# Strassen's seven products in the input projection of a hybrid decoder layer

## The chip, the cores and the metric

The kernel runs on one core of a Trainium2 chip. The metric is the device time of one execution in microseconds. Engines are named as in the profile: PE is TensorE, DVE is VectorE, ACT is ScalarE, POOL is GpSimd, SP is SyncE, whose queue issues the DMA transfers.

## The reference

One layer: a root-mean-square norm of x (1024 tokens by 2048 channels), one combined input projection, three groups of attention heads that read it, a gate on each, an output projection, the residual and a last norm.

```python
h = rmsnorm(x, norm_g) @ w_in
(c_q, c_kv, k_rope, z_mla, q_nsa, k_c, v_c, k_s, v_s, k_w, v_w, g_nsa, z_nsa,
 q_mem, z_mem) = jnp.split(h, offsets, axis=-1)
o_mla = mla_mixer(c_q, c_kv, k_rope, ...) * jax.nn.silu(z_mla)
o_nsa = nsa_mixer(q_nsa, k_c, v_c, k_s, v_s, k_w, v_w, g_nsa, ...) * jax.nn.silu(z_nsa)
o_mem = memory_mixer(q_mem, mem, mem_norm_g, w_mem_kv) * jax.nn.silu(z_mem)
o = jnp.concatenate([o_mla, o_nsa, o_mem], axis=-1) @ w_out
return rmsnorm(x + o, final_norm_g)
```

The projection to 40 feature tiles of 128 columns is what changes. (Some 268 columns that are needed with tokens on the partitions, the "nat" products, are made apart.)

## The kernel before

Every float32 product is made of three: an operand is split into a rounded part `hi` (ACT copies it, L116 or L118) and the remainder `lo` (DVE subtracts, L110 or L112), and `mm3` (L121 to L124) adds hi·hi, hi·lo and lo·hi in PSUM.

**Startup.** For each of the 16 channel tiles of x, ACT and DVE split it into one `big` buffer (16 buffers of 128x2048, all of which then hold x), ACT squares it (L194), POOL adds the square into `acc` (L195), and PE makes the nat products of 128x268. Then come the keys and values of 256 memory tokens, whose squares POOL adds to `macc` (L269). From `acc`, `col_rsqrt` and `spread` make `R`, the inverse norm of every token on all partitions (L229 is its last step).

**Feature tiles.** A loop runs over the 40 feature tiles. A tile takes 16 channel tiles, two halves of 512 tokens and three products: 96 matmuls of 128x512 (L561, `proj_k`) into two of four `S` banks. `wtile` loads half of the tile's weights (512 KB) and splits it; `evac` multiplies each bank by `R` on the way to one of four `work` buffers of 128x1024 (L569 to L573); a SiLU (L575), a split (`keep_split`) or nothing follows, and the result is stored in DRAM. The dictionary `side` lays other work behind given tiles: the compression branch (`kc_...`, `vc_...`), the norms and the scaling of the latent tiles (`c_sum`, `c_norm`, `c_scale`, L467 to L472, which takes two `work` buffers each), the rotary key and memory attention (`mem_...`).

**Order.** Each engine runs its instructions in a fixed order, which a list scheduler makes out of the program's order, the dependencies and the free buffers; SP issues every DMA in one queue. Behind the projection come the loads of the sparse attention: `ks` tiles, `kc`, `qn`, `qrh`, `ali`.

Of the kernel before, what the change touches and what calls it, by code (L numbers as in the profile page):

```python
# [43 lines left out]
def chunks(w):  # L44
    """How w score columns are cut: (first column, columns used, columns computed)."""
    if w <= 512:
        return [(0, w, max(w, 256))]
    f = 384 if w == 640 else 512
    return [(0, f, f), (f, w - f, w - f)]
# [3 lines left out]
def hybrid_block_kernel(ctx: ExitStack, tc, a, out):  # L53
# [16 lines left out]

    def whl():
        return (sb.tile([P, KW], F32R, tag="wh", bufs=4, name=nm("wh"))[:, :1024],
                sb.tile([P, KW], F32R, tag="wl", bufs=4, name=nm("wl"))[:, :1024])
# [47 lines left out]
    def mm3(dst, sh, sl, mh, ml, start, stop):  # L121
        PE.matmul(dst, sh, mh, start=start, stop=False)  # L122
        PE.matmul(dst, sh, ml, start=False, stop=False)  # L123
        PE.matmul(dst, sl, mh, start=False, stop=stop)  # L124

    def rsqrt(dst, v, s, dim):
        """dst = 1 / sqrt(v / dim + EPS); v is overwritten, s is scratch."""
# [17 lines left out]

    cd = [dram(f"c{j}", [P, SEQ]) for j in range(8)]
# [23 lines left out]
    def keep_split(o, dst, n=1024):  # L170
        """Split o and keep both parts in DRAM: dst = (place of hi, place of lo)."""
        hi, lo = work(F32R), work(F32R)
        split(hi[:, :n], lo[:, :n], o)
        store(dst[0], f(hi[:, :n]))
        store(dst[1], f(lo[:, :n]))

    # ------------------------------------------------ input projection
    xt = []
    acc = rs(F32)
    nat = [t[:, :268] for t in (psS(), psS(), psS(), psS(), psT(), psT(), psO(), psJ())]  # L180
    for c in range(8):
# [4 lines left out]
        for k in (2 * c, 2 * c + 1):  # L186
            xr = work()
# [3 lines left out]
            if k == 0:  # L191
                S.activation(acc, xr, AF.Square)
            else:
                S.activation(xr, xr, AF.Square)  # L194
                G.tensor_tensor(acc, acc, xr, op=ALU.add)  # L195
            xt.append(t)
# [6 lines left out]
    vw = [work(), work(), work()]  # L203
    for i in range(NQ):
        d = vw[i // 3][:, (i % 3) * 268:(i % 3) * 268 + 268]
# [6 lines left out]
    def col_rsqrt(col, sq, n, dim):  # L212
        """col[:, i] = the inverse norm of token tile i; sq holds sums of squares along partitions."""
# [5 lines left out]
    def spread(dst, col, n):  # L219
        """dst[:, token] = col of the token, on every partition."""  # L220
# [11 lines left out]
    R = rs(F32)  # L232
# [3 lines left out]
    def nat_out(n):  # L236
        i0 = 3 * n
        m = min(3, NQ - i0)
        for i in range(i0, i0 + m):
            d = vw[n][:, (i - i0) * 268:(i - i0) * 268 + 268]  # L240
            V.tensor_scalar(d, d, rcol[:, i:i + 1], None, op0=ALU.mult)
        v3 = vw[n][:, :m * 268].rearrange("p (i c) -> p i c", c=268)
        S.activation(gates[:, i0:i0 + m, :], v3[:, :, 256:268], AF.Sigmoid)
        hi, lo = whl()
        hi, lo = [t[:, :m * 256].rearrange("p (i c) -> p i c", c=256) for t in (hi, lo)]
        split(hi, lo, v3[:, :, :256])
        for b, dst in enumerate((vsd, vwd)):
            for o, t in ((0, hi), (1024, lo)):
                store(dst[:, o + i0 * P:o + (i0 + m) * P].rearrange("p (i c) -> p i c", c=P), f(t[:, :, b * P:b * P + P]))

    # ------------------------------------------------ memory tokens: keys and values
    macc = sb.tile([P, 256], F32, tag="z", bufs=2, name="macc")
    kps, vps = [psS() for _ in range(4)], [psJ(), psO()]
    for c in range(4):
# [7 lines left out]
        for t in range(4):  # L262
# [7 lines left out]
        for t in range(4):  # L270
            k = 4 * c + t
            wr = wraw()
            load(wr, a["w_mem"][k])
            wh, wl = whl()
            split(wh, wl, wr)
            q = slice(t * 256, t * 256 + 256)
            for h in range(4):
                mm3(kps[h][:, :256], wh[:, h * P:h * P + P], wl[:, h * P:h * P + P],
                    mh[:, q], ml[:, q], k == 0, k == 15)
            for i in range(2):  # L280
                o = t * 256 + i * P
# [1024 lines left out]
```

## Time and profile before

| | us |
|---|---|
| runs | 1959.21, 1960.35, 1960.33 |
| median | 1960.33 |
| span of the profiled execution | 1959.9 |
| projection (first to last L561 matmul) | 125.7 to 1062.9 |

The profiled execution's span, from the first instruction to the last, is 0.4 us below the median of the runs, so spans and times can be compared directly. PE is busy for 98% of the span; DVE, ACT and POOL for 46%, 36% and 9%. The page gives busy time by engine, the costliest groups of instructions with what ended the idle time before them, and the transfers; the trace behind it gives each instruction.

### The profile page before, as it was taken

The page shows a single profiled execution, that of the slowest core. Times are in us where ns is not written, and L with a number is a line of the kernel's source. Part 1 is how long each engine was busy: PE and PEld are TensorE (multiplying, and loading weights), DVE is VectorE, ACT ScalarE, POOL GpSimd, SP SyncE. Part 2 cuts the span into 40 slices and gives each one's busy share as a digit, 9 for nine tenths or more (in the row PEclk, how much of TensorE's full clock was granted, in tenths as well). Part 3 has the DMA queues.
Part 4 walks back from the last instruction along what each step waited for, and adds up shares of the span by engine and source line. Part 5 has one row for each costly group of instructions (what it writes and reads, how often), then busy time and mean ns, then how long its engine had stood idle before and what let it go on. Part 6 is the DMA issues. An engine that isn't in the chain of part 4 may idle for free. (4 is left out here: it accounts for less than half of the span.)

```text
span 1959.9 us, 26350 instructions
## 1 busy us (share of the span) xinstructions
PE 1913.3 (98%) x10174; PEld 1646.6 (84%) x10174; DVE 903.8 (46%) x1908; ACT 705.5 (36%) x1389; POOL 176.9 (9%) x306
## 2 busy tenths in 40 slices
PE   7899999999999999999999999999999999999998
PEld 7788887888888888888887998888998988888888
DVE  8742232333323223222212887858778782244342
ACT  6542231212222112233312666535445462243231
POOL 6400000000100000000000221200000001110120
PEclk9999999999999999999999999999999999999999
DMA  6564443346545243323226234442122165357332
GB/s 211 164 187 128 132 164 116 120 153 224 179 155 189 97 129 97 119 83 108 81 95 183 67 89 137 149 136 63 46 74 63 54 208 173 97 176 275 97 108 87
DMA packets 94683, 255.43 MB, mean 130 GB/s; under 512 B 12059, under 2 KB 37469, under 8 KB 91357
## 3 DMA queue, kind: packets, MB, share of 16 engines
q1 hardware_dynamic: 94557, 253.74, 40.2%
q8 instruction: 80, 1.31, 0.3%
q14 instruction: 46, 0.38, 0.1%
HBM read 190.76 MB, written 62.93 MB: 129 GB/s over the span
## 5 line engine op out<-in xcount | busy, mean ns | idle before, releaser
L561 PE MATMUL S<-big,wh 128*128 128x512 f32 x2560 | 688.9, 391 | 0.0
L561 PEld LDWEIGHTS S<-big,wh 128*128 128x128 f32 x2560 | 477.8, 188 | 97.0
L116 ACT ACTIVATE wh<-wraw 128x1024 fp32r<-128x1024 f32 (+2 forms) x192 | 196.9, 1028 | 711.0 <-PE S L561 393.9
L110 DVE TENSOR_TENSOR wl<-wraw,wh 128x1024 fp32r<-128x1024 f32 (+2 forms) x192 | 246.8, 1289 | 409.5 <-ACT wh L116 407.8
L561 PE MATMUL S<-big,wl 128*128 128x512 f32 x1280 | 396.0, 390 | 0.0
L561 PEld LDWEIGHTS S<-big,wl 128*128 128x128 f32 x1280 | 239.9, 188 | 49.9 <-issue 0.2
L573 DVE TENSOR_TENSOR work<-S,rs 128x512 f32<-128x512 f32 x60 | 38.7, 686 | 295.8 <-PE S L561 295.8
L122 PE MATMUL S<-wh,big 128*128 128x512 f32 (+2 forms) x336 | 122.1, 363 | 7.2 <-ACT big L118 7.2
L124 PE MATMUL S<-wh,big 128*128 128x512 f32 (+2 forms) x336 | 122.5, 365 | 5.3 <-DVE big L112 5.3
L123 PE MATMUL S<-wl,big 128*128 128x512 f32 (+2 forms) x336 | 122.0, 363 | 0.0
L497 ACT ACTIVATE work<-S,st 128x512 f32<-128x512 f32 (+3 forms) x148 | 84.5, 572 | 87.1 <-DVE st L704 33.0
L122 PEld LDWEIGHTS S<-wh,big 128*128 128x128 f32 x336 | 64.4, 192 | 16.6 <-ACT big L118 7.2
L124 PEld LDWEIGHTS S<-wh,big 128*128 128x128 f32 x336 | 64.5, 192 | 15.3 <-DVE big L112 5.8
L122 PE MATMUL O<-wh,big 128*128 128x256 f32 (+2 forms) x232 | 71.3, 307 | 1.2 <-ACT wh L116 1.2
L123 PEld LDWEIGHTS S<-wl,big 128*128 128x128 f32 x336 | 64.4, 192 | 9.3
L123 PE MATMUL O<-wl,big 128*128 128x256 f32 (+2 forms) x232 | 71.5, 308 | 0.1
L1154 POOL TENSOR_TENSOR big<-big,big 128x512 f32<-128x512 f32 (+1 forms) x32 | 42.1, 1344 | 323.2 <-ACT work L1152 321.4
L124 PE MATMUL O<-wh,big 128*128 128x256 f32 (+2 forms) x232 | 71.0, 306 | 0.0
L122 PE MATMUL J<-big,wh 128*128 128x512 f32 x160 | 64.1, 400 | 1.1 <-ACT wh L116 0.9
L123 PE MATMUL J<-big,wh 128*128 128x512 f32 x160 | 63.5, 397 | 0.0
L124 PE MATMUL J<-big,wl 128*128 128x512 f32 x160 | 63.2, 395 | 0.0
L122 PE MATMUL J<-wh,big 128*128 128x256 f32 (+2 forms) x200 | 62.0, 310 | 0.0
(326 smaller groups left out, 3457.0 us busy)
## 6 DMA issues: line engine op xcount, KB each, us to landing
wraw<-in_w_feat SPq DMA_DIRECT2D x80, 512.0 KB, 4.3
wraw<-in_w_o SPq DMA_DIRECT2D x64, 512.0 KB, 3.7
work<-in_xT SPq DMA_DIRECT2D x16, 512.0 KB, 3.7
wraw<-in_w_mem SPq DMA_DIRECT2D x16, 512.0 KB, 4.3
work<-c SPq DMA_DIRECT2D x16, 512.0 KB, 6.2
cs<-work SPq DMA_DIRECT2D x16, 512.0 KB, 3.0
z<-work SPq DMA_DIRECT2D x16, 512.0 KB, 4.6
z<-z SPq DMA_DIRECT2D x64, 128.0 KB, 2.6
```

The lines of the kernel that those rows point to most:

```text
L110: V.tensor_tensor(dst, src, f(hi), op=ALU.subtract)
L116: S.activation(hi, src, AF.Copy)
L122: PE.matmul(dst, sh, mh, start=start, stop=False)
L123: PE.matmul(dst, sh, ml, start=False, stop=False)
L124: PE.matmul(dst, sl, mh, start=False, stop=stop)
L497: S.activation(dst, src, AF.Exp, bias=m, scale=-1.0, accum_out=s)
L561: PE.matmul(A[n], sw[:, kk, :], xt[k][:, off + n * 512:off + (n + 1) * 512], start=(k == 0 and first), stop=(k == KT - 1 and last))
L573: V.tensor_tensor(o[:, h], A[n], R[:, h], op=ALU.mult)
L1154: G.tensor_tensor(y, y, gf[:, c], op=ALU.mult)
```

## The change

The 40 feature tiles become 20 pairs (`units`), and the 16 channel tiles two passes of eight. For each pair and pass, two halves of features, two of channels and two of tokens form a 2x2 by 2x2 block product, which Strassen's scheme (Winograd's form) makes from seven block products in place of eight. A block product is four channel tiles of 128x512 in three matmuls each: 12 matmuls.

For that, the seven sums of blocks of x stand split in `XH` and `XL` (14 of the 16 `big` buffers). In the startup they are made from channel tiles 0 to 7 once `R` is known, since x is now normed ahead of the projection (`normed`) and not behind it. The sums of tiles 8 to 15 are made during pass 1, kept in DRAM (`xd`) and loaded and split at its end (`next_enc`). `wprep` makes the seven weight blocks of a unit: four adds on POOL (128x512), seven splits. `evac` copies two banks and adds five to the outputs, which take two of the four `work` buffers for the unit. Outputs of pass 1 are stored (`c0d`, 1 MB a unit), and in pass 2 they are loaded again and POOL adds them (two adds of 128x1024 a unit). The memory tokens' keys are made in the startup and their values between the passes (`between`), with the remainders of their weights on POOL (`mem_w`). The side work of the projection is laid in pass 2. The number of 128x512 matmuls falls by 480 (40 times 96 is 3840; 20 times 2 times 7 times 12 is 3360).

```diff
+    def slot(dt=F32R):
+        return sb.tile([P, KW], dt, tag="wh", bufs=8, name=nm("wh"))
+
     def whl():
-        return (sb.tile([P, KW], F32R, tag="wh", bufs=4, name=nm("wh"))[:, :1024],
-                sb.tile([P, KW], F32R, tag="wl", bufs=4, name=nm("wl"))[:, :1024])
+        return slot()[:, :1024], slot()[:, :1024]
 
     def wraw():
...
+    c0d = [dram(f"part{u}", [P, 2048]) for u in range(20)]
+    xd = [dram(f"xc{s}", [P, 2048]) for s in range(7)]
...
+    raws = [big(F32) for _ in range(4)]
...
+            xr = raws[k % 4][:, (k // 4) * 1024:(k // 4) * 1024 + 1024] if k < 8 else work()
...
+    def mem_w(name, n):
+        wr = work()
+        load(wr, a[name][n])
+        wh, wl = whl()
+        S.activation(wh, wr, AF.Copy)
+        G.tensor_tensor(wl, wr, f(wh), op=ALU.subtract)
+        return wh, wl
...
+    def enc(s, q, src):
+        o = slice(q * 512, q * 512 + 512)
+        split(XH[s][:, o], XL[s][:, o], src)
+
+    def normed(t, k, half):
+        o = slice(half * 1024, half * 1024 + 1024)
+        V.scalar_tensor_tensor(t[:, o], t[:, o], ng[:, k:k + 1], R, op0=ALU.mult, op1=ALU.mult)
...
+    def wprep(g):
+        u, s = divmod(g, 7)
+        b1, b2 = TX[u]
+        B11, B21, B12, B22 = b1[:, hs[0]], b1[:, hs[1]], b2[:, hs[0]], b2[:, hs[1]]
+        X = tx[:, hs[u % 2]]
+        if s == 1:
+            G.tensor_tensor(B12, B22, B12, op=ALU.subtract)
+            G.tensor_tensor(X, B12, B11, op=ALU.add)
+        if s == 3:
+            G.tensor_tensor(B11, B22, X, op=ALU.subtract)
+            G.tensor_tensor(X, B21, X, op=ALU.subtract)
+        t = slot()
+        split(t[:, :512], t[:, 512:1024], (B11, X, B21, B12, B11, X, B22)[s])
+        W[g] = t
+        if s >= 5 and u + 1 < 2 * NU:
+            raw_load(u + 1, s - 5)
...
+    def product(g):
+        u, s = divmod(g, 7)
+        b = "ababcdc"[s]
+        first = s in (0, 1, 4, 5)
+        if first:
+            banks[b] = psS()
+        w = W.pop(g)
+        for q in range(4):
+            o, m = slice(q * P, q * P + P), slice(q * 512, q * 512 + 512)
+            mm3(banks[b], w[:, o], w[:, 512 + q * P:512 + q * P + P], XH[s][:, m], XL[s][:, m],
+                first and q == 0, q == 3, not first)
+        return banks[b]
...
+    def evac(g, B):
+        u, s = divmod(g, 7)
+        p = u // NU
+        if s == 0:
+            outs[u] = [work(), work()]
+            if p:
+                outs["c0"] = big(F32)
+                load(outs["c0"], c0d[u - NU])
+        o1, o2 = outs[u]
+        C11, C21, C12, C22 = o1[:, hs[0]], o1[:, hs[1]], o2[:, hs[0]], o2[:, hs[1]]
+        if s == 0:
+            S.activation(C21, B, AF.Copy)
+        elif s == 1:
+            V.tensor_tensor(C12, C21, B, op=ALU.add)
+        elif s == 2:
+            S.activation(C11, B, AF.Copy)
+        elif s == 3:
+            V.tensor_tensor(C21, C21, B, op=ALU.add)
+        elif s == 4:
+            V.tensor_tensor(C22, C21, B, op=ALU.add)
+        elif s == 5:
+            V.tensor_tensor(C21, C21, B, op=ALU.add)
+            if p:
+                G.tensor_tensor(o1, o1, outs["c0"][:, :1024], op=ALU.add)
+        else:
+            V.tensor_tensor(C12, C12, B, op=ALU.add)
+            if p:
+                G.tensor_tensor(o2, o2, outs["c0"][:, 1024:], op=ALU.add)
...
+    def post(u, n):
+        p, uu = divmod(u, NU)
+        o, j = outs[u][n], units[uu][n]
+        if not p:
+            store(c0d[uu][:, n * 1024:(n + 1) * 1024], o)
+        elif j >= T_ZMLA:
             S.activation(o, o, AF.Silu)
             store(zd[j - T_ZMLA], o)
         elif j < 8:
...
+    def sums12():
+        for q in Q4:
+            t = raws[q]
+            V.tensor_tensor(t[:, A21], t[:, A21], t[:, A22], op=ALU.add)
+        for q in Q4:
+            t = raws[q]
+            V.tensor_tensor(t[:, A11], t[:, A21], t[:, A11], op=ALU.subtract)
...
+    L = NU - 1
+    at(L, 0, next_in, next_in)
+    at(L, 4, lambda: next_enc(0))
+    at(L, 6, lambda: next_enc(1))
+
+    ne = {0: 2, 2: 3, 3: 4, 5: 5, 6: 6}
+
+    def between():
+        post(L, 0)
+        post(L, 1)
+        for n in range(8):
+            vpair(n)
+            if n in ne:
+                next_enc(ne[n])
+        v_keep()
+
+
+    u0 = NU
...
+    at(u0 + 7, 6, lambda: c_norm(0))
+    at(u0 + 9, 3, lambda: c_norm(1))
     for j in range(4):
-        at(10 + j, lambda j=j: c_scale(j))
-        at(17 + j, lambda j=j: c_scale(4 + j))
-    at(14, k_rope)
+        at(u0 + 9, 3 + j, lambda j=j: c_scale(j))
+        at(u0 + 10, 3 + j, lambda j=j: c_scale(4 + j))
...
+    raw_load(0, 0)
+    raw_load(0, 1)
+    kpair(0)
+    col_rsqrt(rcol, acc, NQ, DM)
+    kpair(1)
+    R = rs(F32)
+    spread(R, rcol, NQ)
+    tx = rs(F32)
+    for q in Q4:
+        normed(raws[q], q, 0)
+    enc_first(0)
+    kpair(2)
+    for q in Q4:
+        normed(raws[q], 4 + q, 1)
...
-    w0_ = wtile(order[0], 0)
-    for n, j in enumerate(order[:-2]):
-        A = [psS(), psS()]
-        w1_ = wtile(j, 1)
-        for k in range(8):
-            proj_k(A, w0_, k)
-        w0_ = wtile(order[n + 1], 0)
-        if n in mid:
-            mid[n]()
-        for k in range(8, 16):
-            proj_k(A, w1_, k)
-        evac(j, A)
-        for fn in side.get(n, []):
...
+    for g in range(14 * NU):
+        u, s = divmod(g, 7)
+        while ready < 14 * NU and ready <= g + (2 if u == 0 else 3):
+            wprep(ready)
+            ready += 1
+        evac(g, product(g))
+        if u > 0 and u != NU and s in (0, 2):
+            post(u - 1, s // 2)
+        for fn in side.pop((u, s), []):
             fn()
-    js = order[-2:]
-    As = [[psS(), psS()], [psS(), psS()]]
-    ws = [w0_, wtile(js[1], 0), wtile(js[0], 1), wtile(js[1], 1)]
-    for k in range(KT):
```

**GpSimd in the startup.** Its queue of the changed kernel, from its third `mem_w` on (`macc`: squares of the memory tokens; L621 and L622: sums of weight blocks; L725: sums of x blocks):

```order
L282 TENSOR_TENSOR wh_932<-work_929,wh_931 128x1024
L274 TENSOR_TENSOR macc<-macc,sq_1050 128x256
L274 TENSOR_TENSOR macc<-macc,sq_1053 128x256
L274 TENSOR_TENSOR macc<-macc,sq_1056 128x256
L274 TENSOR_TENSOR macc<-macc,sq_1059 128x256
L621 TENSOR_TENSOR wraw_765<-wraw_767,rs_890 128x512
L622 TENSOR_TENSOR rs_890<-wraw_765,rs_890 128x512
L725 TENSOR_TENSOR big_181<-big_181 128x512
L282 TENSOR_TENSOR wh_1011<-work_1008,wh_1010 128x1024
L725 TENSOR_TENSOR big_182<-big_182 128x512
L725 TENSOR_TENSOR big_183<-big_183 128x512
L725 TENSOR_TENSOR big_184<-big_184 128x512
```

And before, from the last add of x's squares on:

```order
L195 TENSOR_TENSOR rs_154<-rs_154,work_675 128x1024
L269 TENSOR_TENSOR macc<-macc,sq_749 128x256
L269 TENSOR_TENSOR macc<-macc,sq_752 128x256
L269 TENSOR_TENSOR macc<-macc,sq_901 128x256
L269 TENSOR_TENSOR macc<-macc,sq_904 128x256
L269 TENSOR_TENSOR macc<-macc,sq_907 128x256
L269 TENSOR_TENSOR macc<-macc,sq_910 128x256
```

Behind the squares of x, a queue that held short adds now holds adds and subtractions of 128x512 and 128x1024 between them.

**ScalarE in pass 2, where the latent tiles are scaled.** The changed kernel (`big` from `work`: the hi part of a scaled latent tile; `wh`: weights; L657 and L661: a unit's first and third evacuation, of bank `S_6000`):

```order
L118 ACTIVATE big_5906<-work_5902 128x1024
L118 ACTIVATE wh_6197<-wraw_6040 128x512
L118 ACTIVATE big_5933<-work_5929 128x1024
L118 ACTIVATE big_5963<-work_5959 128x1024
L657 ACTIVATE work_6013<-S_6000 128x512
L118 ACTIVATE big_5990<-work_5986 128x1024
L661 ACTIVATE work_6013<-S_6000 128x512
L118 ACTIVATE wh_6222<-rs_890 128x512
L118 ACTIVATE wh_6245<-wraw_6060 128x512
L118 ACTIVATE big_6080<-work_6076 128x1024
L526 ACT_TABLE_LOAD
L526 ACTIVATE wh_6294,st_6292<-J_6285,st_6292 128x256
```

And before, where the first two latent tiles are scaled (`work_2969` and `work_3099` are their hi parts):

```order
L116 ACTIVATE wh_3109<-wraw_3107 128x1024
L116 ACTIVATE work_2959<-O_2957 64x128
L116 ACTIVATE work_2969<-work_2965 128x1024
L116 ACTIVATE wh_3163<-wraw_3161 128x1024
L116 ACTIVATE wh_3243<-wraw_3241 128x1024
L116 ACTIVATE work_3088<-work_3085 128x1024
L116 ACTIVATE wh_3297<-wraw_3295 128x1024
L116 ACTIVATE work_3099<-work_3095 128x1024
L116 ACTIVATE wh_3377<-wraw_3375 128x1024
```

The scaled tiles stood one to a feature tile, between the splits of the next weights; now four stand close together, and the evacuation of the next unit's first bank stands behind the third of them.

**SyncE's queue at the projection's end.** The changed kernel (`z_155` and `z_156`: the last two gate tiles, after their SiLU; the others: loads for the first scores):

```order
L105 DMA z_155<-work_7842 128x1024
L105 DMA z_156<-work_7843 128x1024
L102 DMA ks_8002<-kc 128x64
L102 DMA ks_8004<-kc 128x64
L102 DMA ks_8003<-kc 128x64
L102 DMA ks_8005<-kc 64x64
...
L102 DMA big_8033<-qn_119 128x2048
L102 DMA big_8035<-qrh_123 64x1024
L102 DMA big_8035<-qrl_125 64x1024
L102 DMA big_8035<-qrh_123 64x1024
L102 DMA big_8035<-ali_137 64x1024
```

And before:

```order
L100 DMA ks_7105<-kc 128x64
L100 DMA ks_7107<-kc 128x64
L100 DMA ks_7106<-kc 128x64
L100 DMA ks_7108<-kc 64x64
L100 DMA big_7138<-qrh_96 64x1024
L100 DMA big_7138<-qrl_98 64x1024
L100 DMA big_7138<-qrh_96 64x1024
L100 DMA big_7138<-ali_110 64x1024
L100 DMA work_7132<-in_cmask 128x512
L100 DMA work_7132<-in_cm 128x64
L103 DMA z_128<-work_7095 128x1024
L103 DMA z_129<-work_7100 128x1024
```

The two stores of the last gate tiles stood behind the loads of the first scores; now they stand ahead of most of them.

## Rows read from the trace of the kernel before

**Rows 1.** The page's first part: busy us (share of the span) and instructions of each engine.

```profile
PE 1913.3 (98%) x10174; PEld 1646.6 (84%) x10174; DVE 903.8 (46%) x1908; ACT 705.5 (36%) x1389; POOL 176.9 (9%) x306
```
**Rows 2.** The page's fifth part, costliest groups: busy, mean ns | idle before, releaser.

```profile
L561 PE MATMUL S<-big,wh 128*128 128x512 f32 x2560 | 688.9, 391 | 0.0
...
L561 PE MATMUL S<-big,wl 128*128 128x512 f32 x1280 | 396.0, 390 | 0.0
```
**Rows 3.** Instructions of L561: duration min/median/max in ns, first and last start.

```profile
L561 PE MATMUL S<-big,wh x2560: 387/390/497, 125.7 to 1062.4; 128*128 128x512 f32 x197
```
**Rows 4.** PE's waits from 130 to 1064 us: total, times, longest.

```profile
PE J L123 <- DVE wl L110: 2.4, 2, 1.7
```
**Rows 5.** Windows, L561 alone: length, PE busy (x), PEld busy (x), PEclk, DMA share, GB/s.

```profile
400.00:500.00 100.00, 100.00 (x443) 82.86 (x442) 1.00 0.60 202
```
**Rows 6.** Windows of the startup: length, PE, PEld, DVE, ACT, POOL, PEclk, DMA, GB/s.

```profile
20.00:25.00 5.00, 5.00 (x41) 4.84 (x40) 4.66 (x4) 3.18 (x5) 2.67 (x2) 1.00 0.79 245
```
**Rows 7.** Timeline around the first attention matmul: start, us, instruction.

```profile
1063.08 0.28 PE L693 MATMUL S<-ks,big 128*128 128x256 f32 x1
1063.20 0.28 PE L694 MATMUL S<-ks,big 128*128 128x256 f32 x1
```
**Rows 8.** Timeline of VectorE and GpSimd in the startup: start, us, instruction.

```profile
10.38 0.71 DVE L110 TENSOR_TENSOR wl<-wraw,wh 128x536 fp32r<-128x536 f32 x1
11.01 1.28 DVE L112 SCALAR_TENSOR_TENSOR big<-work,ng,big 128x1024 fp32r<-128x1024 f32 x1
...
15.55 2.92 DVE L110 TENSOR_TENSOR wl<-wraw,wh 128x536 fp32r<-128x536 f32 x1
...
59.45 5.82 POOL L195 TENSOR_TENSOR rs<-rs,work 128x1024 f32<-128x1024 f32 x2
```
**Rows 9.** Groups by line and shape of GpSimd and VectorE: busy us, mean ns | idle.

```profile
L195 POOL TENSOR_TENSOR rs<-rs,work 128x1024 f32<-128x1024 f32 x15 | 44.4, 2962 | 19.2 <-ACT work L194 18.4
L1154 POOL TENSOR_TENSOR big<-big,big 128x512 f32<-128x512 f32 x24 | 36.2, 1545 | 249.6 <-ACT work L1152 249.6
L458 POOL TENSOR_TENSOR rs<-rs,work 128x1024 f32<-128x1024 f32 x6 | 14.4, 2406 | 359.0 <-ACT work L457 359.0
...
L1154 POOL TENSOR_TENSOR big<-big,big 128x256 f32<-128x256 f32 x8 | 5.9, 742 | 73.6 <-ACT work L1152 71.9 <-DVE st L1128 1.7
...
L573 DVE TENSOR_TENSOR work<-S,rs 128x512 f32<-128x512 f32 x60 | 38.7, 686 | 295.8 <-PE S L561 295.8
...
L110 DVE TENSOR_TENSOR wl<-T,wh 128x256 fp32r<-128x256 f32 x16 | 6.7, 418 | 0.1
```
**Rows 10.** VectorE and ScalarE where the latent tiles are scaled, by line and shape.

```profile
L471 DVE SCALAR_TENSOR_TENSOR work<-work,qg,work 128x1024 f32<-128x1024 f32 x4 | 5.1, 1281 | 11.3 <-DMA work<-c 11.3
...
L110 DVE TENSOR_TENSOR big<-work,big 128x1024 fp32r<-128x1024 f32 x16 | 19.2, 1223 | 11.5 <-ACT big L116 11.5
...
L575 ACT ACTIVATE work<-work 128x1024 f32<-128x1024 f32 x16 | 17.0, 1062 | 43.0 <-DVE work L573 42.9
```
**Rows 11.** Loads of the latent tiles, 200 to 700 us: issue to landing.

```profile
DMA to landing us min/median/max: 2.6/5.6/7.2
```
**Rows 12.** SyncE's timeline at the projection's end: issue start, us, transfers.

```profile
1043.83 2.31 SPq L100 DMA_DIRECT2D ks<-kc  x4
...
1064.11 1.75 SPq L103 DMA_DIRECT2D z<-work  x2
```
**Rows 13.** DMA issues from 1015 to 1066 us: KB each, median us to landing.

```profile
big<-qn SPq DMA_DIRECT2D x1, 1024.0 KB, 7.2
```
**Rows 14.** Windows of PE alone: length, PE busy (x), PEclk, DMA share, GB/s.

```profile
34.00:36.00 2.00, 0.00 (x0) 1.00 0.56 217
36.00:38.00 2.00, 1.45 (x6) 0.52 0.73 190
38.00:40.00 2.00, 2.00 (x13) 0.62 1.06 354
```
**Rows 15.** ScalarE's timeline where the norm has been spread: start, us, instruction.

```profile
87.49 1.07 ACT L229 ACTIVATE rs<-T 128x512 f32<-128x512 f32 x2
```

## What I expect, and why

> **What bounds the kernel now.** I read the page's first part, then its costliest groups, then PE's waits, then single stretches. PE is busy for 98% of the span and DVE, its nearest follower, for 46% [rows 1]: until the projection ends, time is what PE works plus what it waits. The largest item is the 3840 matmuls of L561 [rows 2], from 125.7 to about 1063 us [rows 3]. In 100 us of a stretch without other work 443 of them run [rows 5], one in 0.2257 us. Between 130 and 1064 us PE's largest wait is 2.4 us in two pieces [rows 4], and the first scores start at 1063.08, right behind the projection [rows 7]. So the projection is bound by PE, and a matmul saved there is worth its whole 0.2257 us, as long as PE still finds the next one ready.
>
> The startup is another matter. Its PE work is 384 nat matmuls at 0.122 us (41 in 5 us [rows 6]), 192 memory matmuls of 256 columns at 0.12 us (the distance of the first scores, which are as wide [rows 7]) and 96 of 512 columns: 46.8 + 23.0 + 21.7 = 91.5 us. The projection starts at 125.7, so 34 us are lost to waits and to a slow clock.
>
> **What the change saves.** 480 matmuls of 512 columns: 480 x 0.2257 = **-108.3 us**. Their form is the old one (weights 128x128 loaded for each, 512 columns), so the pitch should hold. The added sums, splits and transfers must hide behind PE, and I went through the stretches asking whether they can.
>
> **Startup: +35.** What I looked for first is what two engines do to each other. From 11.0 us to the last add of squares, which ends at 65.3 [rows 8], DVE made 14 scaled splits of 128x1024 and 6 of 128x536, and POOL 15 adds. Undisturbed these take 1.28 us, 0.71 us [rows 8] and 2.41 us [rows 9]: 17.9 + 4.2 + 36.1 = 58.2 us of work in 54.3 us of time. A DVE subtraction took 2.92 us in place of 0.71 [rows 8], a POOL add 2.96 in place of 2.41 [rows 9]. So a DVE operation with two SBUF inputs and a POOL operation hardly overlap. Evacuations from PSUM stay at 0.69 [rows 9].
>
> The Trainium skill says the same in "SBUF — State Buffer", section "Who interferes with whom": such a DVE instruction and a GpSimd instruction that reads SBUF share a port pair, and the loser blocks for the other's whole length. By the rule alone the startup would be fully serial, 6 us longer than I take it below; the trace agrees to nine tenths, and I go by the trace.
>
> The norm of x cannot be had before the 65.3 us, in either kernel, and now the first product waits for it. From there to the last product of the first unit the order holds, on DVE, 44 splits and sums of 512 columns (0.70), 8 of 1024 (1.28) and 12 of 256 (0.42 [rows 9]): 46 us; on POOL, 8 remainders of 1024 (2.41), 14 adds of 256 (0.74) and 12 of 512. The last appear in no row: between half of 2.41 and the 1.545 of a multiply [rows 9], I take 1.4. POOL: 19.3 + 10.4 + 16.8 = 46.5. Together 92.5, at nine tenths 86. With 2.7 us for the last product (12 x 0.2257) and 4 us of gaps while the norm is spread, the first unit ends near 65.3 + 86 + 7 = 158. PE's work until then is 46.8 + 23.0 + 84 x 0.2257 = 88.8, so 69 us are lost where 34 were. If nothing excluded anything, the norm (ready at 88.6 before [rows 15]) and DVE's own 46 us would end the unit near 137 (+14); with all serial and longer gaps, 178 (+55).
>
> **The rest of pass 1: +4.** A unit is 84 matmuls, 19.0 us. DVE needs 7 splits and 5 evacuations (8.3 us), POOL four adds (about 5.6), ACT less than DVE: covered by PE. The first units still share DVE with the late pieces of the startup; 0 to 8.
>
> **Between the passes: +12.** PE has the values' 96 matmuls (21.7 us). Against them stand five `next_enc` on DVE, ten splits at 1.22 [rows 10], 16 splits of memory tokens at 0.42, one remainder (1.2), and 8 remainders of 2.41 on POOL: 12.2 + 6.7 + 1.2 + 19.3 = 39.4 us that exclude each other, 18 more than PE has; the preparation that ran ahead hides some. If they did overlap, 3; at worst 22.
>
> **Pass 2, usual units: +6.** POOL adds two outputs of 1024: 10.4 us a unit, with DVE's 7 splits 15.3, with a kept split of two outputs 17.7, still under 19.0. Where the compression branch and the squares of latent tiles come on top it is close; 0 to 12.
>
> **Pass 2, scaling of the latent tiles: +25.** Before, a scaling was laid behind each of eight feature tiles, with `work` buffers free. Now a unit's outputs hold two of the four, a scaling takes two, and eight scalings stand in two units. So a pair is loaded, scaled, split and only then the next loaded: a load lands in 2.6 to 7.2 us [rows 11], then 1.28 for the product and 1.22 for the remainder [rows 10], and 0.8 for two issues, 6 to 10 us a round. ScalarE's order shows who is late: the copy of the next unit's first bank stands behind the hi part of the third scaled tile. Three rounds at 8 us are 24; PE has four banks, that is four products or 10.8 us, before it must stop: 13 lost. The second group has four rounds, 32 us, against the end of one unit and four products of the next, some 20: 12 lost. With loads at 2.6 us it is 10 in all, with 7.2 it is 45; I take the middle of the rounds.
>
> **The projection's end: +15.** Before, SP had issued the loads of the first scores long before they were needed (the `kc` pieces at 1043.83) and the last two stores, at 1064.11, came behind them [rows 12]. Now those stores stand ahead of `kc` and `qn`. The last store waits for the last evacuation (0.69), POOL's add (2.41) and a SiLU (1.06 [rows 10]): 4.2 us behind the last product. Then four `kc` pieces take 2.3 [rows 12], some six issues more at 0.45, and `qn` lands 7.2 us after its issue [rows 13]: 16 us, a little less with less traffic. Bounds 10 and 18.
>
> **Clock: +7.** After the idle stretch around 34 to 36 us the granted clock is 0.52 and 0.62 in the next two windows of 2 us [rows 14], near the lower of its two levels (1.2 and 2.4 GHz): 0.48 x 2 + 0.38 x 2 = 1.7 us lost. The startup's loss above includes this. Four new stalls (between the passes, two at the scalings, one at the end) make 7; 0 if they come as short waits.
>
> **Sum.** -108.3 + 35 + 4 + 12 + 6 + 25 + 15 + 7 = -4.3. The profiled span of 1959.9 becomes 1955.6; the median lies 0.4 above the span, so **1956 us**.
>
> **Rivals.** *The cover holds* (rival A). Startup +20, between the passes +4, units +8, scalings +10, end +12, clock +5: -49, about 1911. For it speaks that the stalls were summed one by one, though an engine that runs ahead in one stall has less to do at the next; against it, that the startup's serial chain hangs on a measured exclusion. Range 1890 to 1940.
>
> *POOL and DVE become the bound of pass 2* (rival B), the side that ends slower. If POOL's add of 512 takes more than about 1.7 us in company, a unit with a kept split has 4 x 1.7 + 4.8 + 4.9 + 2.4 = 19 us of mutually exclusive work, as much as PE has; beyond it PE waits for weights in each such unit. At 2.5 us in each of the twelve units with kept splits, compression or scaling: +30, about 1986. For it speaks that a POOL add in company took 2.96 against 2.41 [rows 9]; against it, that a loser's wait is the winner's work, already counted. Range 1978 to 2010.
>
> That the change would not do what it says I leave out: the matmul counts are fixed by the program.
>
> **How the numbers follow.** My sum holds within about 20 us: 1940 to 1978, chance 0.48. Rival A has 0.26, rival B 0.26. Leaving out a tenth on each side cuts four tenths of either rival's range: 1909 to 1996. A measurement of this kernel tells 0.2%, 3.9 us, from no change: the border lies at 1956.4 and 1964.2. Of the middle case 16.4 of 38 us lie below, which gives 0.21, plus 0.26: faster 0.47; between the borders 0.10; above 0.17 + 0.26 = 0.43.
>
> **What would show it.** Right: 3360 matmuls in the product's line at the old pitch; first unit ending near 158 us, DVE and POOL alternating before it; a gap of PE of over 10 us behind four products where ACT's copy waits on a scaled tile's load; a gap of some 15 us between the last product and the first scores, ended by a DMA. Wrong: PE dense from the second unit to the scores (rival A), or PE waiting 1 to 3 us for `wh` in most units of pass 2 (rival B). A pitch above 0.23 us would overthrow the first term.

## The result, and the profile after

The changed kernel takes 2060.27 us (median of 4 runs, 2059.35 to 2063.76); the kernel before took 1959.77, timed beside it. The ratio is 1.0514, with a 95% interval of 1.0493 to 1.0534: 5.1% slower. The forecast was 1956 us with a range up to 1996, so it missed by 104 us.

The page's engine line and the costliest group of the changed kernel, to be held against [rows 1] and [rows 2]:

```profile
span 2061.9 us, 27060 instructions
...
PE 1855.9 (90%) x9694; PEld 1576.5 (76%) x9694; DVE 1210.6 (59%) x2291; ACT 859.6 (42%) x1721; POOL 594.1 (29%) x546
...
L124 PE MATMUL S<-big,wh 128*128 128x512 f32 x1120 | 451.0, 403 | 78.6 <-ACT work L657 51.5
```

PE's busy share fell from 98% to 90%, POOL's rose from 9% to 29%. L124 is the first of `mm3`'s three lines; with L125 and L126 it makes the 3360 matmuls that replace L561, and before it PE now waits, where L561 waited for nothing. Where, the windows of three stretches show (length, then busy us and instructions of PE, PEld, DVE, ACT and POOL, granted clock, DMA share, GB/s):

```profile
280.00:520.00 240.00, 239.73 (x1057) 198.50 (x1058) 110.14 (x154) 66.72 (x112) 69.85 (x51) 1.00 0.32 110
617.00:848.00 231.00, 200.96 (x878) 157.01 (x877) 112.16 (x156) 86.97 (x130) 101.63 (x57) 0.93 0.54 180
848.00:974.00 126.00, 75.31 (x313) 60.23 (x312) 64.20 (x77) 35.13 (x58) 32.80 (x18) 0.78 0.72 250
```

The first lies in pass 1 (units 6 to 18): PE never stops, and a unit of 84 matmuls takes 19.0 us, as computed. The second is pass 2 with the compression branch, the third the scaling of the latent tiles, where PE works 60% of the time and the granted clock sinks to 0.78.

For every kernel below I worked out from its trace how much PE **lost** in a stretch: the stretch's length less its matmuls, each at its columns x 0.2257/512 us (a narrower one counted as 64). A unit ends with its 84th product matmul, so units 0 to 19 are pass 1 (unit 0 with the startup) and 20 to 39 pass 2 (unit 20 with the values between the passes). In us:

| kernel | startup, unit 0 | 1-6 | 7-19 | 20 | 21-29 | 30-32 | 33-39 | gap before scores | median |
|---|---|---|---|---|---|---|---|---|---|
| the changed kernel | 71.5 | 18.5 | 1.1 | 17.3 | 60.1 | 62.6 | 21.7 | 19.7 | 2060.27 |
| spread | 70.6 | 16.5 | 1.1 | 16.0 | 56.8 | 9.4 | 45.2 | 19.6 | 2029.08 |
| chunk_big | 71.2 | 17.1 | 1.1 | 15.7 | 53.9 | 61.8 | 23.6 | 19.5 | 2054.97 |
| stores_last | 71.3 | 16.3 | 1.1 | 17.3 | 59.6 | 61.9 | 19.3 | 13.3 | 2051.64 |
| dve_adds | 55.9 | 8.8 | 1.1 | 6.2 | 30.6 | 57.9 | 9.5 | 17.8 | 1979.86 |
| pool_idle | 75.5 | 18.7 | 1.1 | 18.3 | 62.3 | 65.5 | 27.0 | 21.4 | 2087.65 |
| dve_spread | 55.9 | 11.0 | 1.1 | 7.5 | 33.3 | 4.3 | 27.0 | 18.6 | 1946.73 |
| no_pool | 41.0 | 7.0 | 1.1 | 9.3 | 25.9 | 3.3 | 24.3 | 13.9 | 1918.82 |
| np_both | 41.0 | 6.8 | 1.1 | 7.7 | 16.8 | 4.1 | 22.6 | 13.3 | 1911.90 |
| np_loads | 42.3 | 8.7 | 1.1 | 9.3 | 20.3 | 4.9 | 23.7 | 3.2 | 1909.27 |

Before, the startup lost 35.5 and the projection 24.4, 59.9 together. In the changed kernel the row's sum is 272.5: 212.6 more, less the 108.3 that the matmuls saved, is 104.3. The spans differ by 102.0, since what follows the first scores ran 2.2 us shorter. So the account closes: the saving came, and twice of it was lost again.

PE's longest waits after (total, times, longest), against [rows 4]:

```profile
PE S L124 <- ACT work L657: 51.5, 7, 17.8
PE S L927 <- DMA big<-qn: 19.7, 1, 19.7
PE O L126 <- POOL wh L282: 15.0, 7, 5.5
PE T L563 <- DVE wh L554: 15.0, 7, 7.5
```

They name the copy of a unit's first bank, the queries' load, GpSimd's remainder of memory weights and the softmax of memory attention. None names what proved the largest cause, since it stretches instructions and does not release them.

### The profile page after: what moved, and what is told of

The parts are those of the page before. It is cut to its first block, busy times and chain, and to the rows that moved or that the text cites. A ratio compares the mean times of both kernels' runs of the same rounds, so it can differ in the third digit from the quotient of the medians.

```text
span 2061.9 us, 27060 instructions
## 1 busy us (share of the span) xinstructions
PE 1855.9 (90%) x9694; PEld 1576.5 (76%) x9694; DVE 1210.6 (59%) x2291; ACT 859.6 (42%) x1721; POOL 594.1 (29%) x546
## 5 line engine op out<-in xcount | busy, mean ns | idle before, releaser
L124 PE MATMUL S<-big,wh 128*128 128x512 f32 x1120 | 451.0, 403 | 78.6 <-ACT work L657 51.5
L125 PE MATMUL S<-big,wh 128*128 128x512 f32 x1120 | 446.0, 398 | 2.3 <-DVE big L112 2.3
L112 DVE TENSOR_TENSOR wh<-wraw,wh 128x512 fp32r<-128x512 f32 (+3 forms) x296 | 296.0, 1010 | 257.5 <-ACT wh L118 250.9
L126 PE MATMUL S<-big,wh 128*128 128x512 f32 x1120 | 444.9, 398 | 1.7 <-DVE wh L112 1.5
L118 ACT ACTIVATE wh<-wraw 128x512 fp32r<-128x512 f32 (+3 forms) x296 | 217.4, 746 | 387.1 <-PE S L126 129.7
L124 PEld LDWEIGHTS S<-big,wh 128*128 128x128 f32 x1120 | 215.9, 193 | 131.7 <-ACT work L657 54.8
L126 PEld LDWEIGHTS S<-big,wh 128*128 128x128 f32 x1120 | 215.9, 193 | 49.6 <-DVE wh L112 3.9
L125 PEld LDWEIGHTS S<-big,wh 128*128 128x128 f32 x1120 | 216.2, 193 | 45.5 <-DVE big L112 3.2
L618 POOL TENSOR_TENSOR wraw<-wraw 128x512 f32<-128x512 f32 x40 | 53.6, 1339 | 340.3 <-DMA wraw<-in_w_feat 322.2
L124 PE MATMUL S<-wh,big 128*128 128x512 f32 (+2 forms) x336 | 121.2, 362 | 6.8 <-ACT big L120 6.7
L126 PE MATMUL S<-wh,big 128*128 128x512 f32 (+2 forms) x336 | 120.7, 364 | 6.1 <-DVE big L114 5.5
L125 PE MATMUL S<-wh,big 128*128 128x512 f32 (+2 forms) x336 | 120.9, 361 | 0.0
L112 DVE TENSOR_TENSOR wh<-rs,wh 128x512 fp32r<-128x512 f32 x80 | 69.0, 862 | 81.3 <-ACT wh L118 80.6
L1285 POOL MEMSET wh<- 128x128 f32 x64 | 13.8, 228 | 292.1 <-PE O L125 167.5
L622 POOL TENSOR_TENSOR rs<-wraw,rs 128x512 f32<-128x512 f32 x40 | 56.6, 1415 | 83.5 <-DVE wh L112 83.1
L621 POOL TENSOR_TENSOR wraw<-wraw,rs 128x512 f32<-128x512 f32 x40 | 58.8, 1470 | 67.1 <-DVE wh L112 66.1
L126 PEld LDWEIGHTS S<-wh,big 128*128 128x128 f32 x336 | 63.0, 190 | 17.7 <-DVE big L114 8.2
L124 PEld LDWEIGHTS S<-wh,big 128*128 128x128 f32 x336 | 63.8, 190 | 16.4 <-ACT big L120 7.0
L112 DVE TENSOR_TENSOR wh<-T,wh 128x512 fp32r<-128x512 f32 (+2 forms) x112 | 61.5, 570 | 18.5 <-ACT wh L118 18.4
```

Source lines behind the costliest of these rows:

```text
L112: V.tensor_tensor(dst, src, f(hi), op=ALU.subtract)
L118: S.activation(hi, src, AF.Copy)
L124: PE.matmul(dst, sh, mh, start=start, stop=False, skip_group_check=shared)
L125: PE.matmul(dst, sh, ml, start=False, stop=False, skip_group_check=shared)
L126: PE.matmul(dst, sl, mh, start=False, stop=stop, skip_group_check=shared)
L618: G.tensor_tensor(B12, B22, B12, op=ALU.subtract)
```

## Experiments

The theories were: **1**, the four `work` buffers and queues that stand behind a scaling; **2**, exclusion of DVE and POOL (rival B of the prediction, and more than that); **3**, the three `wraw` buffers, which the compression weights share with the projection's.

**spread.** One scaling to a unit.

```diff
-    for j in range(4):
-        at(u0 + 9, 3 + j, lambda j=j: c_scale(j))
-        at(u0 + 10, 3 + j, lambda j=j: c_scale(4 + j))
-    at(u0 + 11, 3, k_rope)
+    for j in range(8):
+        at(u0 + 9 + j, 3, lambda j=j: c_scale(j))
+    at(u0 + 17, 3, k_rope)
```

> The eight scalings of latent tiles one to a unit (units 29 to 36 of 40) in place of four in each of two units, the rotary key behind them; nothing else is changed. Theory 1 (a round of load, scale, split, store takes 10 us because a scaling and a unit's outputs share four work buffers, and the next unit's first copy queues behind it): units 30 to 32, which lost 62.7 us together, lose under 15, the time falls by 45 to 55 us. Theory 2 (DVE and POOL exclude each other and are the bound of pass 2): the same work is done, so the time falls by under 10 us.

Measured: 2029.08 us (ratio 1.0354, 1.0324 to 1.0384), 31 us below the changed kernel, where 45 to 55 were expected. Units 30 to 32 lost 9.4 in place of 62.6, as theory 1 had it, but units 33 to 39, which now carry five of the scalings beside memory attention, lost 23.5 more. ScalarE's timeline of the changed kernel (start, us, instruction) shows the rounds:

```profile
904.30 1.06 ACT L118 ACTIVATE big<-work 128x1024 fp32r<-128x1024 f32 x1 [3.37 <-issue]
...
914.80 1.06 ACT L118 ACTIVATE big<-work 128x1024 fp32r<-128x1024 f32 x1 [5.83 <-DVE work L499]
924.50 1.06 ACT L118 ACTIVATE big<-work 128x1024 fp32r<-128x1024 f32 x1 [8.64 <-DVE work L499]
925.46 0.58 ACT L657 ACTIVATE work<-S 128x512 f32<-128x512 f32 x1
```

In this second group of four a scaled tile follows the other by 10 us, and the copy of bank `S` (L657), for which PE waits, comes only behind the last of them. DVE's and SyncE's timelines of the same place say what fills a round:

```profile
913.43 1.28 DVE L499 SCALAR_TENSOR_TENSOR work<-work,kvg,work 128x1024 f32<-128x1024 f32 x1 [3.74 <-DMA work<-c]
...
923.13 1.28 DVE L499 SCALAR_TENSOR_TENSOR work<-work,kvg,work 128x1024 f32<-128x1024 f32 x1 [6.01 <-DMA work<-c]
```

```profile
914.75 0.32 SPq L102 DMA_DIRECT2D work<-r  x1
915.88 1.58 SPq L105 DMA_DIRECT2D cs<-big  x2
917.51 0.72 SPq L102 DMA_DIRECT2D work<-c  x1
```

The next tile's load is issued at 917.51, behind the stores of the last one, and its product starts at 923.13: load, product, split, store, one after the other.

**dve_adds.** DVE does the change's additions.

```diff
-        G.tensor_tensor(wl, wr, f(wh), op=ALU.subtract)
+        V.tensor_tensor(wl, wr, f(wh), op=ALU.subtract)
...
-            G.tensor_tensor(B12, B22, B12, op=ALU.subtract)
+            V.tensor_tensor(B12, B22, B12, op=ALU.subtract)
...
-                G.tensor_tensor(o1, o1, outs["c0"][:, :1024], op=ALU.add)
+                V.tensor_tensor(o1, o1, outs["c0"][:, :1024], op=ALU.add)
```

(and so the other sums of weight and x blocks)

> Every add and subtraction that the change put on POOL (remainders of the memory weights, sums of weight blocks and of x blocks, the adds of pass 1's outputs) is done by DVE; POOL keeps the squares. Theory 2 (DVE and POOL exclude each other): DVE needs half of POOL's time for the same, so all stretches before pass 2 gain: the startup loses 50 us in place of 71, units 1 to 6 lose 5 in place of 18, the stretch between the passes 10 in place of 17, and pass 2 some 10 less; in all 40 to 50 us faster. Theory 1 (buffers and queues): only the startup gains, 20 us, and pass 2 stays within 5 us. If the two engines did not exclude each other, DVE's longer queue would make it slower.

Measured: 1979.86 us (1.0103, 1.0073 to 1.0132), 80 us below the changed kernel, twice what theory 2 had forecast. The table's row shows it in every stretch but units 7 to 19 (nothing) and 30 to 32 (5 us): the startup 16 less, units 1 to 6 ten, unit 20 eleven, units 21 to 29 thirty, units 33 to 39 twelve. Two groups by shape, of the changed kernel and then of this one (busy us, mean ns), show why:

```profile
L112 DVE TENSOR_TENSOR wh<-wraw,wh 128x512 fp32r<-128x512 f32 x200 | 173.5, 877 | 52.0 <-ACT wh L118 45.7 <-DMA xc<-big 5.8
...
L663 DVE TENSOR_TENSOR work<-work,S 128x512 f32<-128x512 f32 x40 | 27.4, 685 | 48.5 <-PE S L126 48.5
```

```profile
L112 DVE TENSOR_TENSOR wh<-wraw,wh 128x512 fp32r<-128x512 f32 x200 | 137.4, 696 | 43.2 <-ACT wh L118 41.6
...
L663 DVE TENSOR_TENSOR work<-work,S 128x512 f32<-128x512 f32 x40 | 27.4, 685 | 38.4 <-PE S L126 38.4
```

The remainder of a weight block, two inputs in SBUF, takes 877 ns beside GpSimd and 696 without it. The evacuation of the same size, one input in SBUF and one in PSUM, takes 685 in both. (The prediction's row for this came from the old projection, in which GpSimd was at work for 19 of 937 us.) The Trainium skill states in "SBUF — State Buffer", section "Who interferes with whom", that a DVE instruction with two SBUF inputs contends with a GpSimd instruction that reads SBUF, and that one with at most one SBUF input, outside the 2-port modes, does not. With this rule the trace agrees, by these numbers.

The same holds for DVE's instructions together. I took each of them up to the last product less the undisturbed duration of its shape (that of the fastest tenth in no_pool, before_no_pool and the changed kernel). Those with two SBUF inputs were stretched by 138 us in the changed kernel, 41 in dve_adds and, to go ahead of the next runs, 171 in pool_idle and 6 in no_pool; all others by 3 to 12 us.

**pool_idle.** On top of dve_adds, GpSimd makes adds that nothing reads:

```diff
+    def idle_adds(src, n):
+        for i in range(n):
+            G.tensor_tensor(idle, src[:, :256], src[:, 256:512], op=ALU.add)
...
             V.tensor_tensor(X, B12, B11, op=ALU.add)
+            idle_adds(B22, 4)
```

> The kernel of dve_adds, and beside it GpSimd makes adds of 128x256 that nothing reads, at the places of its former work: eight a unit in place of the four sums of weight blocks, three for each remainder of memory weights and for each add of pass 1's outputs. No matmul waits for their results. If what the 81 us paid for is the exclusion itself (DVE blocked while GpSimd reads), half or more of them come back: 40 us or more, in the startup, between the passes and in pass 2. If it is GpSimd's own slowness in the chain from a load to a weight, under 15 us come back.

Measured: 2087.65 us (1.0633, 1.0605 to 1.0662), 108 us above dve_adds (104 by the ratios, since the kernel before, timed beside it, ran 4 us slower). More came back than had been saved, and DVE's remainder rose again:

```profile
L281 POOL TENSOR_TENSOR idle<-wraw 128x256 f32<-128x256 f32 x320 | 347.8, 1087 | 383.1 <-DMA wraw<-in_w_feat 360.9
```

```profile
L112 DVE TENSOR_TENSOR wh<-wraw,wh 128x512 fp32r<-128x512 f32 x200 | 166.5, 841 | 39.0 <-ACT wh L118 38.5
```

The losses of units 1 to 6, 20 and 21 to 29 are those of the changed kernel within 2.5 us. No matmul needs a result of these adds, so GpSimd's own slowness in the chain is not needed for the loss; that it is at work is enough. What the slowness added in the changed kernel is not separated. Two reservations: DVE here does GpSimd's old work too, so more of it is exposed, and the adds hold their source buffers longer. For the second, the load queue waited 19 us for them up to the first scores, of the 104 (total, times, longest):

```profile
SPq L102 <- POOL idle L281: 19.1, 10, 8.5
```

**chunk_big.** The compression weights leave `wraw` (shown for the values; `kc_chunk` likewise):

```diff
-        wr = wraw()
-        load(wr, a["w1v"][c])
+        if c % 2 == 0:
+            cmp_["raw"] = big(F32)
+            for n in range(2):
+                load(cmp_["raw"][:, 1024 * n:1024 * n + 1024], a["w1v"][c + n])
+        o = 1024 * (c % 2)
```

> The raw weights of the compression branch are loaded two pieces at a time into a free big buffer, so that the three wraw buffers hold only the projection's own weights. Theory 3 (units 21 to 28, which lost 50 us together, lose them because compression weights and the next unit's weights wait for the same three wraw buffers in one queue): they lose under 25, the time falls by 25 us or more. Theory 2: under 5 us.

Measured: 2054.97 us (1.0486, 1.0456 to 1.0517), 5 us below the changed kernel, where theory 3 had 25 or more; units 21 to 29 lost 53.9 in place of 60.1. Theory 3 is a side matter.

**stores_last.** `post` of the last unit moved behind the loads of the first scores:

```diff
-    post(2 * NU - 1, 0)
-    post(2 * NU - 1, 1)
...
     qn = nsa_q(0)
+    post(2 * NU - 1, 0)
+    post(2 * NU - 1, 1)
```

> The SiLU and the stores of the last two gate tiles stand behind the loads of the first scores in the program, so in SyncE's queue too; nothing else is changed. Expected: the gap of 19.7 us ahead of the first scores falls to under 5, the time falls by 14 to 19 us. If the loads were late for another reason (their buffers), the gap stays.

Measured: 2051.64 us (1.0469, 1.0439 to 1.05), 9 us less, with the gap at 13.3. A third of the gap was the stores; a miss for the rest. In the changed kernel SyncE's end of the projection, against [rows 12], reads:

```profile
1148.76 3.67 SPq L105 DMA_DIRECT2D z<-work  x2
1152.48 2.28 SPq L102 DMA_DIRECT2D ks<-kc  x4
...
1157.99 0.43 SPq L102 DMA_DIRECT2D big<-qn  x1
```

and PE's, where [rows 7] had no wait:

```profile
1167.51 0.55 PE L927 MATMUL S<-ks,big 128*128 128x256 f32 x1 [19.66 <-DMA big<-qn]
```

**dve_spread** joins dve_adds and spread.

> The kernel of dve_adds with the eight scalings one to a unit. Units 30 to 32, which lost 58 us in dve_adds, lose under 15; some of it comes back in units 33 to 37: 30 to 45 us faster than dve_adds, 1935 to 1950 us, which is below the kernel before (1959.5). If exclusion was what made the scalings slow, the gain is under 15 us.

Measured: 1946.73 us (0.9911, 0.9894 to 0.9928), 33 us below dve_adds (38 by the ratios) and 0.9% below the kernel before. Units 30 to 32 lose 4.3: the serial rounds and the exclusion are two causes, and their gains (31 and 80 us, 114 together) add.

**no_pool.** dve_spread and stores_last, and DVE does the squares' adds and the rotary product too:

```diff
-                G.tensor_tensor(acc, acc, sq, op=ALU.add)
+                V.tensor_tensor(acc, acc, sq, op=ALU.add)
```

> The kernel of dve_spread with the squares' adds (of x, of the memory tokens, of the latent tiles) and the rotary product on DVE as well, and the last two gate stores behind the loads of the first scores. From exclusion: the 15 adds of x's squares cost 1.23 us each on DVE in place of 2.41 on a shared path, so the first unit ends 10 to 15 us earlier; 4 us at the latent norms; 6 to 9 at the scores: 18 to 28 us below dve_spread. If DVE is now the bound of the startup by its own work, the startup gains nothing.

Measured: 1918.82 us (0.9772, 0.9758 to 0.9787), 28 us below dve_spread. The first unit ends at 128.4 us; it ended at 159.2 in the changed kernel and at 143.6 in dve_adds.

**before_no_pool.** The same for the kernel before, its only edit:

> The kernel before with its squares' adds and its rotary product on DVE in place of GpSimd, nothing else. If exclusion slows the startup of both kernels alike, its projection starts 8 to 13 us earlier than at 125.7 and the time falls to about 1949; if not, DVE's longer queue leaves it the same or slower.

Measured: 1940.55 us (0.9884, 0.9869 to 0.9898), 23 us below the kernel before. The projection starts at 107.7, against [rows 3]:

```profile
L561 PE MATMUL S<-big,wh x2560: 387/389/497, 107.7 to 1042.0; 128*128 128x512 f32 x197
```

So the adds of squares, the fifteen of [rows 9] and those of the memory tokens, had cost the old kernel's startup 18 us. And what Strassen's scheme is worth where GpSimd is out of the projection in both kernels is the difference of no_pool and this one: 21.7 us of the 108.3, with the scalings and the last stores of no_pool placed anew as well.

**np_chunk, np_early, np_both** are no_pool with the edit of chunk_big, with memory attention a unit earlier (`g = 71` in place of `g = 78`), and with both.

> The kernel of no_pool with the raw compression weights in a big buffer (as in chunk_big). Units 22 to 28 lost 24 us in no_pool. If the shared wraw buffers are what is left there, they lose under 14, the time falls by 8 to 12 us; chunk_big alone gave 6 while exclusion was still there. If what is left is the small matmuls' own inefficiency, no change (2 us).

> The kernel of no_pool with memory attention laid seven products (one unit) earlier, so that its last output is stored a unit before the projection's end. In stores_last the last of these stores still waited in SyncE's queue for 9.8 us ahead of the loads of the first scores. Expected: the gap ahead of the first scores falls from 13.9 to under 5 us, the time by 8 to 10 us. If the loads wait for the x buffers that the last products read, the gap stays over 10.

> The kernel of no_pool with both edits, compression weights in a big buffer and memory attention a unit earlier. If the two are independent, their gains add: 1900 to 1906 us.

Measured: 1916.68 (0.9775, 0.9749 to 0.9802), 1923.25 (0.981, 0.9791 to 0.9828) and 1911.9 us (0.9759, 0.9729 to 0.9789). np_chunk's runs (1914.21 to 1920.95) span no_pool's, though units 21 to 29 lost 20.1 in place of 25.9. np_early is a miss: the gap stayed at 13.8, so the last attention output's store had not been what held the loads. Its units 33 to 39 lost 34.0 in place of 24.3; the cause is open, since np_both has memory attention at the same place and lost 22.6. np_both was expected at 1900 to 1906. What stood ahead of the query load in np_early, SyncE's timeline shows:

```profile
999.13 0.42 SPq L102 DMA_DIRECT2D ks<-ks  x1
...
1009.34 0.32 SPq L102 DMA_DIRECT2D big<-kw  x1
...
1017.36 0.33 SPq L102 DMA_DIRECT2D big<-qn  x1
```

From the first key load to `qn` the queue takes 18 us, and `qn` stands behind 20 others.

**np_loads.** np_both with the queries' loads first and the values' last (the function `nsa_q` moves ahead with its call):

```diff
+    qn = nsa_q(0)
     kh_ = [sb.tile([P, KW], F32R, tag="wh", bufs=8, name=nm("ks")) for _ in range(2)]
...
-    vs, vw_ = big(), big()
-    load(f(vs), vsd)
-    load(f(vw_), vwd)
...
-    qn = nsa_q(0)
+    vs, vw_ = big(), big()
+    load(f(vs), vsd)
+    load(f(vw_), vwd)
```

> The kernel of np_both with the loads of the first scores in another order: queries, their rotary parts and distances first, then keys, and the values of the sparse attention last. The first scores need queries and keys but no values, and the order of np_early held the query load behind 20 issues, each of which waited its turn in the queue. If the place in the queue is what made it late, the gap ahead of the first scores falls from 13.3 to under 7 us and the time by 5 to 9 us, to about 1904. If the transfers themselves are the limit (some 6 MB between the last buffers' release and the scores), the gap only moves to another load.

Measured: 1909.27 us (0.9726, 0.9702 to 0.975). The gap closed to a wait on the last key piece:

```profile
PE S L940 <- DMA ks<-kc: 3.2, 1, 3.2
```

So the place in the queue made `qn` late. But the time hardly moved, where 5 to 9 us were expected: its runs (1905.62 to 1913.46) and np_both's (1907.85 to 1917.81) overlap. In the profiled executions the first scores start at 1008.3 us in np_loads and at 1008.4 in np_both: the 10 us won in the gap had been lost in the stretches ahead of it (the table's rows; 3.5 of them in units 21 to 29), and from the first scores to the end it took 902.1 us where np_both took 897.7. Why is not known. It is the fastest median of the study, 2.7% below the kernel before.

## Why the prediction was wrong

**Right: the saving.** The 84 matmuls of a unit take 19.0 us in units 7 to 19; the -108.3 stood.

**Right: the startup, +35.** The first unit was to end near 158 and ended at 159.2; it lost 71.5 where 35.5 were lost before, +36. DVE's four scaled tiles there took 2.2 us each in place of 1.28:

```profile
81.91 8.80 DVE L599 SCALAR_TENSOR_TENSOR big<-big,ng,rs 128x1024 f32<-128x1024 f32 x4 [1.51 <-ACT rs L234]
```

Here the two engines' work was counted as one sum with no PE time to hide it, and that is the right way to count it: from the last add of x's squares, at 67.7, to the unit's end one or the other was at work in 88.3 of 91.5 us.

**Right mechanism, size off: the scalings, +25.** The place, the serial rounds and the stop behind four products, until ACT's copy, came as described. But a round of the second group took 10 us, my upper bound, where I had taken 8, and PE's two long waits, 13 and 12 in my sum, were 16.5 and 17.8:

```profile
876.02 0.80 PE L124 MATMUL S<-big,wh 128*128 128x512 f32 x1 [16.45 <-ACT work L657]
...
926.09 0.80 PE L124 MATMUL S<-big,wh 128*128 128x512 f32 x1 [17.79 <-ACT work L657]
```

With shorter waits and the low clock, three units lost 62.6; spread gives back 53 of them there.

**Roughly right: between the passes +12** (17.3 lost) **and the projection's end +15** (19.7). At the end the reason was half right: the stores made 6 of it, and the order of the loads 10 of the 13 that were left (stores_last, np_loads).

**Wrong: usual units +6, "still under 19.0" and "it is close; 0 to 12".** This step failed, and with it "covered by PE" for the first units (+4). I added up the mutually exclusive work of a unit without side work, 15.3 to 17.7 us, held it against PE's 19.0 and called it hidden; for the compression branch and the squares of the latent tiles, which come on top, I added up nothing. Units 21 to 29 lost 60.1 and units 1 to 6 18.5, and dve_adds took back 30 and 10 of these, with 11 in unit 20 and 12 in units 33 to 39. Unit 21, the only one of 21 to 29 without such side work, lost 1.4. What PE waited for in these nine units (total, times, longest) was the copy of a unit's first bank, the compression weights, and a sum that waits for GpSimd's squares:

```profile
PE S L124 <- ACT work L657: 10.9, 3, 5.2
PE J L124 <- ACT wh L118: 9.7, 9, 2.5
PE T L221 <- POOL rs L486: 6.4, 1, 6.4
```

The missing sum can be estimated from the instructions in the trace at their undisturbed durations. In units 28 and 29 the exclusive work is 50 us against 41 of PE's: 23.5 were lost, in dve_adds 12.4. In units 22 to 24 it is 54 against 66, and yet 17.3 were lost, in dve_adds 5.8. So in part the sum was incomplete, and in part a sum below PE's time does not hide. It did hide in units 7 to 19, which lost nothing in any kernel, pool_idle's included. That a DVE which already starts late, for a load or a buffer, hands each stretch on to all that is queued behind it, the evacuations too, is the likely reason; no run isolates it.

**Rival B** named this mechanism, with 1986 us and a range that ended at 2010. Its condition, an add of 512 on GpSimd above 1.7 us, did not come: the four sums of weight blocks took 1.34 to 1.47 us in the mean, and it was above all DVE's instructions that were stretched.

```profile
L621 POOL TENSOR_TENSOR wraw<-wraw,rs 128x512 f32<-128x512 f32 x40 | 58.8, 1470 | 67.1 <-DVE wh L112 66.1
```

Its objection, "a loser's wait is the winner's work, already counted", is not refuted by pool_idle, since the idle adds are exclusive work too (14 in a unit of pass 2, at 0.74 us each 10 us). It helps only where the sum is complete and hides.

**Size off: the clock, +7.** From unit 20 on the granted clock falls again and again behind PE's waits; in the old projection it stood at 1.00. The whole stretch up to the last product, and the old projection:

```profile
0.00:1147.80 1147.80, 982.93 (x4534) 803.23 (x4534) 660.82 (x828) 447.94 (x715) 489.95 (x282) 0.94 0.54 182
125.70:1063.20 937.50, 933.83 (x4310) 774.72 (x4309) 261.15 (x357) 218.25 (x277) 18.72 (x15) 1.00 0.42 135
```

An estimate from the trace, PE's busy time weighed with what the granted clock then lacked of full speed, gives 41 us up to the last product, of which 10 lie in the startup (6 before), 13 in units 21 to 29 and 9 in 30 to 32. Against the 7 stand 30 outside the startup; they are part of the losses in the table, and dve_adds (25 by the same estimate) gained partly by them.

**The sum.** Predicted extra losses were 104 us, measured 212.6. Of the difference, 51 lie in pass 2's usual units (81.8, less the 24.4 that the kernel before lost in its projection, where 6 were forecast), 38 at the scalings, 16 in pass 1, 5 at each end of pass 2 and 1 in the startup, less the 7 that I had set down for the clock beside them. Another slip moved nothing: four tenths off rival B's range of 1978 to 2010 leave 1997, not 1996. What part of units 21 to 29 remains (26 us in no_pool, 17 in np_both) was not traced further; the kernel before also loses 24.4 over its whole projection.

## What to carry to other kernels

Count what two engines do exclusively as work of one engine, with all the side work of the stretch, and don't hold the sum against another engine's time only: ask whether the stretch has slack at every point. Before moving an elementwise operation to GpSimd, see whether DVE's neighbours have two SBUF inputs; here doing it all on DVE was 80 us faster, and 23 us faster in the kernel that had seemed tuned. A scheme that saves PE work pays only what its preparation leaves: 21.7 of 108.3 us here, and only once scalings and additions were placed anew.

## What was not expected of the hardware

GpSimd's adds cost DVE time even when they stand outside every chain: 488 idle adds of 128x256, about 1.1 us each, made the kernel over 100 us slower. In units 7 to 19 the same adds stretched DVE's two-input instructions by 21 us and cost nothing: pool_idle and dve_adds both lost 1.1 us there. Single instructions are stretched much further than the means tell: in the changed kernel's startup one remainder of a weight block took 2.43 us that takes 0.69 alone.

```profile
139.13 2.43 DVE L112 TENSOR_TENSOR wh<-rs,wh 128x512 fp32r<-128x512 f32 x1 [0.21 <-ACT wh L118]
```
